# Two of eight key blocks of one query half take their bias on TensorE ahead of exp, in an attention kernel with a shared bias

## The chip, the cores and the metric

One core of a Trainium2 chip. The metric is the device time of one execution in microseconds, given as the median over several executions of one kernel; a profile's span is about 1.8 us shorter than the time of the same execution (247.7 against 249.47 us for the kernel before). Engines: PE multiplies matrices, ACT (ScalarE) does exp, DVE (VectorE) multiplies and copies, POOL (GpSimd) and SP issue transfers.

## The reference

```python
# q, k, v: [4, 8, 1024, 64] float32, bias: [1, 1, 1024, 1024] float32
scores = scale * np.matmul(q, k.transpose(0, 1, 3, 2)) + bias      # scale = 1/8
attn = exp(scores - max) / (sum(exp(scores - max)) + 1e-8)          # over the keys
return np.matmul(attn, v)
```

32 heads, and one bias for all of them. The kernel leaves the maximum out and uses exp(s + b) = exp(s) * exp(b), so that exp(b) is made once and multiplied in for every head.

## The kernel before

The scores of one head are cut into *banks* of 128 keys x 512 queries: 16 pairs of heads x 2 heads x 2 query halves x 8 key blocks = 512 banks. Three banks make a *slot*: PE fills it with three matmuls, ACT does one exp over all three. Two slots are in flight. The values' accumulators and the transposes of q and k share the two PSUM banks that remain.

```python
banks = [(pr, h, qh, kc) for pr in range(NP) for qh in range(2) for kc in range(NCH) for h in range(2)]
banks[NB - 16:] = [(NP - 1, h, 1, kc) for h in range(2) for kc in range(NCH)]
late_bias = {NB - 2: 0, NB - 1: 1}            # only these two banks get their bias on PE
slots = [[0], [1, 2]] + [list(range(i, min(i + 3, NB))) for i in range(3, NB, 3)]
# ... cut
def s_fill(g):                                # PE: scores of a slot
    # ... cut: ps is the slot's PSUM tile
    for j, b in enumerate(slots[g]):
        pr, h, qh, kc = banks[b]
        nc.tensor.matmul(ps[:, j, :], kT[:, kc, :], qT[:, h, qh * HQ:(qh + 1) * HQ],
                         start=True, stop=b not in late_bias)
        if b in late_bias:                    # adds bias / scale: identity x braw
            nc.tensor.matmul(ps[:, j, :], ident[:], braw[:, late_bias[b], :], start=False, stop=True)

def s_exp(g):                                 # ACT: exp(scale * scores) of a slot
    nc.scalar.activation(e_at(slots[g][0], n), open_ps.pop(("S", g))[:, :n, :], ACTF.Exp, scale=scale)
# b_fill / b_exp: four "bias slots" early on: PE transposes the bias, ACT makes eb = exp(bias)
def mul_pair(b, n=2):                         # DVE: E *= eb for 2 or 4 banks
    # ... cut
    nc.vector.tensor_tensor(e, e, eb[:, qh, kc:kc + 1, :].to_broadcast([P, n, HQ]), op=ALU.mult)
# av_bank: PE, four matmuls of 65 columns per bank: values and row sums
# transpose_pe: PE, eight transposes make a quarter of a pair's qT or kT; DVE copies it out (a "piece")
```

The order of all this is fixed at build time: a small list scheduler with guesses of each cost decides in which order each engine gets its instructions. Every engine then runs its own list strictly in that order. The last loads of the start are issued so:

```python
load_v(0)
for c in (QC, QC + 2):
    nc.gpsimd.dma_start(out=btraw[:, c:c + 2, :], in_=bf_[:, c:c + 2, :])   # bias of query half 1
load_qk(1)                                                                   # k and q of pair 1
load_v(1)
```

The softmax here doesn't subtract the row's maximum and nothing guards it: scores larger than these inputs give would overflow.

## Time and profile before

| | before |
|---|---|
| time, median of 3 | 249.73 us (249.12 to 250.07) |
| span of the profile | 247.7 us |
| busy: ACT, PE, DVE | 239.8, 229.4, 218.8 us |
| one exp of three banks, from end to end | 1.343 us |

Two habits of reading are needed. Busy time is a union, so the cost of one of many overlapping instructions is read from the step between neighbours, not from the mean length. And an engine whose ends are modelled (PE) looks busy while it waits. For ACT I go one step further than the page: I take the end of each activation from the trace. In the kernel before, every exp of three banks ends 1.343 us after its predecessor and each of the four bias exps 1.770, from the first three-bank exp (ends at 9.32 us) to the last slot (243.00 us). Whatever exceeds these steps I call a *stall*. A *fill* is the run of matmuls that PE issues for one slot. The lines that carry this are in the prediction.

### The profile page before, as it was taken

The page shows a single profiled execution, that of the slowest core. Times are in us where ns is not written, and L with a number is a line of the kernel's source. Part 1 is how long each engine was busy: PE and PEld are TensorE (multiplying, and loading weights), DVE is VectorE, ACT ScalarE, POOL GpSimd, SP SyncE. Part 2 cuts the span into 40 slices and gives each one's busy share as a digit, 9 for nine tenths or more (in the row PEclk, how much of TensorE's full clock was granted, in tenths as well). Part 3 has the DMA queues.
Part 4 walks back from the last instruction along what each step waited for, and adds up shares of the span by engine and source line. Part 5 has one row for each costly group of instructions (what it writes and reads, how often), then busy time and mean ns, then how long its engine had stood idle before and what let it go on. Part 6 is the DMA issues. An engine that isn't in the chain of part 4 may idle for free.

```text
span 247.7 us, 7189 instructions
## 1 busy us (share of the span) xinstructions
PE 229.4 (93%) x3153; PEld 140.9 (57%) x3153; DVE 218.8 (88%) x381; ACT 239.8 (97%) x183; POOL 54.8 (22%) x76
## 2 busy tenths in 40 slices
PE   8669999999999999999999999999999999999893
PEld 3246656656565665665656555566565555665452
DVE  4118899999999999999999999999998999998884
ACT  5899999999999999999999999999999999999993
POOL 7664534202213501303240031516000000000000
PEclk9999999999999999999999999999999999999999
DMA  6999999923925994922992049699901102020111
GB/s 116 187 202 189 200 146 192 92 85 45 149 55 101 136 81 122 91 89 30 176 132 78 17 91 123 87 130 117 127 16 42 46 0 89 3 85 3 52 57 65
DMA packets 48751, 23.79 MB, mean 96 GB/s; under 512 B 34512, under 2 KB 44624, under 8 KB 48720
## 3 DMA queue, kind: packets, MB, share of 16 engines
q0 software_dynamic: 42560, 14.42, 53.8%
q1 hardware_dynamic: 5872, 8.72, 9.8%
q8 instruction: 24, 0.39, 0.6%
q10 hardware_dynamic: 288, 0.20, 0.3%
q14 instruction: 7, 0.06, 0.1%
HBM read 29.36 MB, written 8.39 MB: 152 GB/s over the span
## 4 chain that ended last, share of the span: by engine, by line
ACT 75%; PE 12%; DVE 7%; issue 2%; DMA 2%; POOL 1%; ACTq 0%; POOLq 0%
ACT E L137 72%; PE ps L130 9%; ACT eb L150 3%; DVE E L163 2%; PE po L188 2%; DMA kr<-in_k_dram 2%; DVE E L160 1%; DVE E L157 1%; DVE oall L200 1%; PE px L89 1%; DVE qT L98 1%; DVE rs L198 0%; DVE kT L102 0%; POOL qT L260 0%; POOL qT L261 0%
## 5 line engine op out<-in xcount | busy, mean ns | idle before, releaser
L137 ACT ACTIVATE E<-ps 128x1536 bf16<-128x1536 f32 (+2 forms) x172 | 230.1, 1666 | 1.0 <-PE ps L130 1.0
L130 PE MATMUL ps<-qT,kT 128*128 128x512 bf16 x512 | 138.7, 378 | 9.8 <-ACT E L137 5.6
L188 PEld LDWEIGHTS <-E 128*128 128x128 bf16 x2016 | 82.0, 98 | 40.2 <-DVE E L160 3.8
L160 DVE TENSOR_TENSOR E<-E,eb 128x2048 bf16<-128x2048 bf16 x78 | 93.9, 1216 | 4.2 <-ACT eb L150 4.0
L188 PE MATMUL po<-vall,E 128*128 128x65 bf16 x2016 | 92.7, 194 | 2.2 <-DVE E L160 1.3
L130 PEld LDWEIGHTS <-kT 128*128 128x128 bf16 x512 | 45.0, 97 | 41.9 <-issue 10.6
L163 DVE TENSOR_TENSOR E<-E,eb 128x1024 bf16<-128x1024 bf16 x92 | 61.0, 684 | 1.9 <-ACT E L137 1.4
L75 POOL DMA_DIRECT2D kr<-in_k_dram x15 | 10.5, 701 | 87.7 <-PE px L89 85.8
L98 DVE TENSOR_TENSOR qT<-px,mask 128x1024 bf16<-128x1024 bf16 x31 | 21.3, 688 | 8.7 <-PE px L89 8.0
L81 POOL DMA_DIRECT2D vall<-in_v_dram x32 | 28.2, 884 | 3.5 <-DVE kT L317 3.1
L200 DVE TENSOR_TENSOR oall<-po,rs 128x256 f32<-128x256 f32 x63 | 26.7, 424 | 2.2
L76 POOL DMA_DIRECT2D qr<-in_q_dram x15 | 10.8, 717 | 26.2 <-PE px L89 22.8
L102 DVE COPY kT<-px 128x512 bf16<-128x512 bf16 x30 | 12.6, 420 | 1.6 <-PE px L89 1.2
L198 DVE RECIPROCAL rs<-po 128x4 f32<-128x4 f32 x63 | 11.1, 176 | 2.4 <-PE po L188 2.2
L89 PE MATMUL px<-ident,qr 128*64 128x128 bf16 x248 | 12.8, 225 | 0.0
L89 PE MATMUL px<-ident,kr 128*64 128x128 bf16 x240 | 12.4, 224 | 0.2
L89 PEld LDWEIGHTS <-qr 128*64 128x64 bf16 x248 | 7.9, 109 | 7.6 <-issue 5.1
L89 PEld LDWEIGHTS <-kr 128*64 128x64 bf16 x240 | 7.7, 109 | 6.9 <-issue 4.5
L150 ACT ACTIVATE eb<-pb 128x2048 bf16<-128x2048 bf16 x4 | 7.5, 1887 | 0.0
L145 PEld LDWEIGHTS <-btraw 128*128 128x128 bf16 x64 | 4.5, 145 | 1.5 <-issue 1.2
L145 PE MATMUL pb<-ident,btraw 128*128 128x128 bf16 x64 | 4.5, 224 | 0.8 <-ACT E L137 0.5
L157 DVE TENSOR_TENSOR E<-E,eb 128x1024 bf16<-128x1024 bf16 (+2 forms) x7 | 4.6, 686 | 0.2 <-ACT E L137 0.2
(45 smaller groups left out, 27.3 us busy)
## 6 DMA issues: line engine op xcount, KB each, us to landing
out_dram<-oall SPq DMA_DIRECT2D x28, 256.0 KB, 2.0
vall<-in_v_dram POOLq DMA_DIRECT2D x32, 128.0 KB, 5.9
kr<-in_k_dram POOLq DMA_DIRECT2D x15, 256.0 KB, 4.2
qr<-in_q_dram POOLq DMA_DIRECT2D x15, 256.0 KB, 4.8
btraw<-in_bias_dram POOLq DMA_DIRECT2D x4, 512.0 KB, 7.9
out_dram<-oall SPq DMA_DIRECT2D x7, 128.0 KB, 3.1
k0f<-in_k_dram SPq DMA_DIRECT2D x2, 128.0 KB, 3.0
q0f<-in_q_dram ACTq DMA_DIRECT2D x1, 128.0 KB, 2.5
```

The source lines that it names most:

```text
L81: nc.gpsimd.dma_start(out=vall[:, 2 * pr + t, :, :D], in_=vf[pr, :, t])
L89: nc.tensor.transpose(px[t * D:(t + 1) * D, c, :], src[:, t, half * QC + c, :], ident[:])
L98: nc.vector.tensor_tensor(dst[:, :, half * HQ:(half + 1) * HQ], px.rearrange("p c q -> p (c q)").unsqueeze(1).to_broadcast([P, 2, HQ]), ma ...
L102: nc.vector.tensor_copy(dst[:, half * QC:(half + 1) * QC, :], px[:])
L130: nc.tensor.matmul(ps[:, j, :], kT[:, kc, :], qT[:, h, qh * HQ:(qh + 1) * HQ], start=True, stop=b not in late_bias)
L137: nc.scalar.activation(e_at(slots[g][0], n), open_ps.pop(("S", g))[:, :n, :], ACTF.Exp, scale=scale)
L150: nc.scalar.activation(eb[:, qh, :, c0 * P:(c0 + 2) * P], open_ps.pop(("B", qh, c0))[:, :NCH].rearrange("p k c q -> p k (c q)"), ACTF.Exp)
L160: nc.vector.tensor_tensor(e, e, eb[:, qh, kc:kc + 2, :].unsqueeze(2).to_broadcast([P, 2, 2, HQ]), op=ALU.mult)
L163: nc.vector.tensor_tensor(e, e, eb[:, qh, kc:kc + 1, :].to_broadcast([P, n, HQ]), op=ALU.mult)
L188: nc.tensor.matmul(acc[:, i, :], e[:, 0, i * P:(i + 1) * P], vall[:, 2 * pr + h, kc, :], start=(kc == 0 and i == 0), stop=(kc == NCH - 1), ...
L198: nc.vector.reciprocal(rs[:], acc[:, :, D:D1])
L200: nc.vector.tensor_tensor(oall[:, c0:c0 + QC, :], acc[:, :, :D], rs[:].to_broadcast([P, QC, D]), op=ALU.mult)
```

## The change

Its intent: in the second query half, key blocks 6 and 7 of all heads get their bias from PE ahead of exp (an identity matmul that adds it), as the last two banks did already. exp(bias) isn't needed there, so two bias slots shrink from 8 to 6 key blocks, and DVE doesn't multiply these 64 banks. They are spread so that a slot has at most one of them until the very last slot. The cost guesses and the order of the early loads change with it.

```diff
+    NE = NCH - 2
+    for u in range(16, NB, 32):
+        early = [(u // 32, h, 1, kc) for kc in range(NE) for h in range(2)]
+        late = [(u // 32, h, 1, kc) for kc in range(NE, NCH) for h in range(2)]
... cut: the first unit also takes banks of pair 1 in, the last has its own order
+        b = u
+        while b < u + 16:
+            if late and (b % 3 == 2 and (u + 16 < NB or b < NB - 8) or not early):
+                banks[b] = late.pop(0)
+                b += 1
+            else:
+                banks[b:b + 2] = early[:2]
+                del early[:2]
+                b += 2
+    late_bias = {b: banks[b][3] - NE for b in range(NB) if banks[b][2] == 1 and banks[b][3] >= NE}
... s_fill: the bias matmuls follow the slot's three score matmuls
+        for j, b in enumerate(slots[g]):
             if b in late_bias:
                 nc.tensor.matmul(ps[:, j, :], ident[:], braw[:, late_bias[b], :], start=False, stop=True)
... b_fill and b_exp
-        nc.scalar.activation(eb[:, qh, :, c0 * P:(c0 + 2) * P],
-                             open_ps.pop(("B", qh, c0))[:, :NCH].rearrange("p k c q -> p k (c q)"), ACTF.Exp)
+        n = NE if qh else NCH
+        nc.scalar.activation(eb[:, qh, :n, c0 * P:(c0 + 2) * P],
+                             open_ps.pop(("B", qh, c0))[:, :n].rearrange("p k c q -> p k (c q)"), ACTF.Exp)
... loads
-        for c in (QC, QC + 2):
-            nc.gpsimd.dma_start(out=btraw[:, c:c + 2, :], in_=bf_[:, c:c + 2, :])
+        nc.gpsimd.dma_start(out=btraw[:, QC:QC + 2, :], in_=bf_[:, QC:QC + 2, :])
         load_qk(1)
+        nc.gpsimd.dma_start(out=btraw[:, QC + 2:, :], in_=bf_[:, QC + 2:, :])
... the scheduler's guesses
-        EXP, EXP0, QK, AV, TP = 427, 62, 216, 170, 350
+        EXP, EXP0, QK, AV, TP = 427, 62, 216, 140, 440
-        for at, x in ((3, (0, 0)), (5, (0, 2)), (9, (1, 0)), (11, (1, 2))):
+        for at, x in ((3, (0, 0)), (5, (0, 2)), (8, (1, 0)), (11, (1, 2))):
```

More of the change, by code (lines that the diff above doesn't have):

```diff
@@ L107 @@
     NB = len(banks)
-    banks[NB - 16:] = [(NP - 1, h, 1, kc) for h in range(2) for kc in range(NCH)]
-    late_bias = {NB - 2: 0, NB - 1: 1}
+    NE = NCH - 2
+    for u in range(16, NB, 32):
+        early = [(u // 32, h, 1, kc) for kc in range(NE) for h in range(2)]
+        late = [(u // 32, h, 1, kc) for kc in range(NE, NCH) for h in range(2)]
+        if u == 16:
+            early += [(1, h, 0, kc) for kc in range(NCH) for h in range(2)]
+            b = 16
+            while b < 48:
+                if late and b % 3 == 2 and b > 36:
+                    banks[b] = late.pop(0)
[4 more added lines that the diff above has]
+                    b += 2
+            continue
+        if u + 16 == NB:
+            early = [(NP - 1, h, 1, kc) for h in range(2) for kc in range(NE)]
+            late = [(NP - 1, h, 1, kc) for h in range(2) for kc in range(NE, NCH)]
+        b = u
+        while b < u + 16:
+            if late and (b % 3 == 2 and (u + 16 < NB or b < NB - 8) or not early):
+                banks[b] = late.pop(0)
+                b += 1
+            else:
+                banks[b:b + 2] = early[:2]
+                del early[:2]
+                b += 2
+    assert sorted(banks) == sorted((pr, h, qh, kc) for pr in range(NP) for h in range(2) for qh in range(2) for kc in range(NCH))
+    late_bias = {b: banks[b][3] - NE for b in range(NB) if banks[b][2] == 1 and banks[b][3] >= NE}
+    units = {}
+    for b in range(NB):
+        units.setdefault(banks[b][:3], []).append(b)
     slots = [[0], [1, 2]] + [list(range(i, min(i + 3, NB))) for i in range(3, NB, 3)]
@@ L143, in b_fill @@
         for c in range(2):
-            for kc in range(NCH):
+            for kc in range(NE if qh else NCH):
                 nc.tensor.transpose(ps[:, kc, c, :],
@@ L163, in mul_pair, with late_bias_pe @@
             nc.vector.tensor_tensor(e, e, eb[:, qh, kc:kc + 1, :].to_broadcast([P, n, HQ]), op=ALU.mult)
-    def late_bias_pe(tag):
-        px = ps_x.tile([P, 2, HQ], BF, tag=tag, name="px")
-        for j in range(2):
-            for i in range(QC):
-                nc.tensor.transpose(px[:, j, i * P:(i + 1) * P],
-                                    btraw[:, QC + i, :].rearrange("p (kp kc) -> p kc kp", kc=NCH)[:, NCH - 2 + j, :],
-                                    ident[:])
+    def late_bias_pe(j, tag):
+        px = ps_x.tile([P, HQ], BF, tag=tag, name="px")
+        for i in range(QC):
+            nc.tensor.transpose(px[:, i * P:(i + 1) * P],
+                                btraw[:, QC + i, :].rearrange("p (kp kc) -> p kc kp", kc=NCH)[:, NE + j, :], ident[:])
         def copy():
-            nc.vector.tensor_scalar(braw[:], px[:], 1.0 / scale, None, op0=ALU.mult)
+            nc.vector.tensor_scalar(braw[:, j, :], px[:], 1.0 / scale, None, op0=ALU.mult)
         return copy
@@ L182, in av_bank @@
         pr, h, qh, kc = banks[b]
-        if kc == 0:
+        first, last = (b == units[pr, h, qh][i] for i in (0, -1))
+        if first:
             po[h] = ps_x.tile([P, QC, D1], F32, tag=tag, name="po")
@@ L188, in av_bank @@
             nc.tensor.matmul(acc[:, i, :], e[:, 0, i * P:(i + 1) * P], vall[:, 2 * pr + h, kc, :],
-                             start=(kc == 0 and i == 0), stop=(kc == NCH - 1), skip_group_check=True)
-        if kc < NCH - 1:
+                             start=(first and i == 0), stop=last, skip_group_check=True)
+        if not last:
             return None
@@ L340 @@
         x_unit = {}
-        bias_at = {(0, 0): 10900, (0, 2): 13700, (1, 0): 18600, (1, 2): 20800}
-        raw_at = {0: (5900, 12600), 1: (22200, 23500), 2: (26000, 28500)}
+        bias_at = {(0, 0): 10900, (0, 2): 13700, (1, 0): 18600, (1, 2): 23300}
+        raw_at = {0: (5900, 12600), 1: (19600, 20900), 2: (26000, 28500)}
         pieces = [(0, 0, 1)]
@@ L345 @@
             pieces += [(pr, 1, 0), (pr, 0, 0), (pr, 1, 1), (pr, 0, 1)]
-        pieces.append((NP, 0, 0))
-        raw_at[NP] = (T0, T0)
+        pieces[4:4] = [(NP, 0, j) for j in range(NCH - NE)]
+        raw_at[NP] = (23400, 23400)
         piece_end = {(0, 1, 0): T0, (0, 0, 0): T0, (0, 1, 1): T0 + 200}
@@ L355 @@
         for u in range(0, NB, 16):
-            if u + 16 < NB:
-                av_order += [u + 2 * i for i in range(8)] + [u + 2 * i + 1 for i in range(8)]
-            else:
-                av_order += list(range(u, NB - 8))
+            for h in range(2):
+                av_order += units[banks[u][0], h, banks[u][2]]
+        del av_order[NB - 8:]
         av_next = 0
@@ L373, in cost_act @@
             item = order[i]
-            return EXP0 + EXP * (len(slots[item[1]]) if item[0] == "S" else 4)
+            return EXP0 + EXP * (len(slots[item[1]]) if item[0] == "S" else NE / 2 if item[1] else 4)
         def act_end_of(i):
@@ L392, in pe_fill @@
                     pr, h, qh, kc = banks[b]
-                    for key in ((pr, 1, kc // QC), (pr, 0, qh)) + (((NP, 0, 0),) if b in late_bias else ()):
+                    for key in ((pr, 1, kc // QC), (pr, 0, qh)) + (((NP, 0, late_bias[b]),) if b in late_bias else ()):
                         if key not in piece_end:
@@ L419, in pe_piece @@
             at = slots[order[i][1]][0]
-            if at < (pr - 2) * 32 + 8:
+            if pr < NP and at < (pr - 2) * 32 + 8:
                 return None
@@ L425, in pe_piece @@
             tags = sorted((x_free[x], x) for x in x_free if x != busy)
-            if busy and left < 4 and at < pr * 32 - 16:
+            if busy and left < 4 and pr < NP and at < pr * 32 - 16:
                 return None
-            if not busy and av_next and at < pr * 32 - 16 and tags[0][0] + SEM < t_pe and len(tags) > 1 and tags[1][0] > t_pe:
+            if not busy and av_next and pr < NP and at < pr * 32 - 16 and tags[0][0] + SEM < t_pe and len(tags) > 1 and tags[1][0] > t_pe:
                 return None
@@ L431, in pe_piece @@
             ready = max(free + SEM, raw_at[pr][1 - which])
-            cost_t = TP if pr < NP else 720
+            cost_t = TP
             def emit(t):
                 pieces.pop(0)
-                copy = transpose_pe(pr, which, half, tag) if pr < NP else late_bias_pe(tag)
-                cost = COPYK if which else COPYQ
+                copy = transpose_pe(pr, which, half, tag) if pr < NP else late_bias_pe(half, tag)
+                cost = COPYK if which or pr == NP else COPYQ
                 x_free[tag] = 1e12
@@ L500, in pe_av @@
             u = unit_of(b)
-            if banks[b][3] == 0:
+            if b == units[u][0]:
                 free, tag = min((x_free[x], x) for x in x_free)
@@ L521, in pe_pick @@
             f = pe_fill()
+            bare = not f and len(filled) < NO and order[len(filled)][0] == "S"
             best = None
@@ L530, in pe_pick @@
                 limit = max(act_end_of(i - 2) + SEM, act_end_of(i - 1) - 830)
-            for c in (pe_piece(), pe_av()):
+            for is_av, c in enumerate((pe_piece(), pe_av())):
                 if c is None:
@@ L534, in pe_pick @@
                 start = max(t_pe, c[0])
-                if start + pe_cost(start, c[1]) > limit and not force:
+                if start + pe_cost(start, c[1]) > limit and not force and (is_av or not bare):
                     continue
@@ L551, in dve_pick @@
                     ready = max(exp_at[b + n - 1], eb_at[(qh, kc)]) + SEM
-                    if n == 2 and b % 4 == 0 and b + 3 in exp_at and (qh, kc + 1) in eb_at and b + 3 not in late_bias and \
+                    if n == 2 and b >= 32 and b % ET <= ET - 4 and [x[1:] for x in banks[b:b + 4]] == \
+                            [(y, qh, kc + x) for x in range(2) for y in range(2)] and b + 3 in exp_at and (qh, kc + 1) in eb_at and b + 3 not in late_bias and \
                             exp_at[b + 3] + SEM <= max(t_dve, ready) and \
@@ L566, in run @@
                         mul_next += n
+                        while mul_next in late_bias:
+                            mul_next += 1
                     c.append((ready, 2, cost, run))
```

## The prediction

> **What bounds the kernel now.** I read the engine totals first, then the slices, then the groups, and then the order of time, because a share of busy time does not say which engine the others wait for.
>
> ```profile
> PE 229.4 (93%) x3153; PEld 140.9 (57%) x3153; DVE 218.8 (88%) x381; ACT 239.8 (97%) x183; POOL 54.8 (22%) x76
> ...
> PE   8669999999999999999999999999999999999893
> ...
> DVE  4118899999999999999999999999998999998884
> ACT  5899999999999999999999999999999999999993
> ...
> L137 ACT ACTIVATE E<-ps 128x1536 bf16<-128x1536 f32 (+2 forms) x172 | 230.1, 1666 | 1.0 <-PE ps L130 1.0
> L130 PE MATMUL ps<-qT,kT 128*128 128x512 bf16 x512 | 138.7, 378 | 9.8 <-ACT E L137 5.6
> L188 PE MATMUL po<-vall,E 128*128 128x65 bf16 x2016 | 92.7, 194 | 2.2 <-DVE E L160 1.3
> L160 DVE TENSOR_TENSOR E<-E,eb 128x2048 bf16<-128x2048 bf16 x78 | 93.9, 1216 | 4.2 <-ACT eb L150 4.0
> L163 DVE TENSOR_TENSOR E<-E,eb 128x1024 bf16<-128x1024 bf16 x92 | 61.0, 684 | 1.9 <-ACT E L137 1.4
> ```
>
> Three engines show nines nearly everywhere, but only ACT has no idle time: its 172 exps of scores sat idle before for 1.0 us in all, and that was in the first 8 us. The score matmuls on PE wait for ACT (5.6 us), hardly ACT for PE. The mean of 1666 ns is not the price of an exp, since one overlaps the next; the price is the step in the chain of waits, read in order of time (start, us, what):
>
> ```profile
> 13.35 1.77 ACT eb L150
> 15.12 1.34 ACT E L137
> 16.46 1.77 ACT eb L150
> 18.23 4.03 ACT E L137 x3
> 22.26 1.77 ACT eb L150
> 24.03 1.34 ACT E L137
> 25.38 1.77 ACT eb L150
> ```
>
> An exp of three score banks takes 1.34 us, an exp of a bias slot (2048 elements) 1.77 us. From 9.3 us to the end of the last exp at 243.0 us the sum is 168 x 1.343 (three banks) + 4 x 1.77 + 0.92 (the last slot, two banks) = 233.6: the stretch itself. There is not a tenth of a microsecond of slack on ACT to win back. What follows, 243.0 to 247.7, is the last attention-value matmuls, a division and the output DMA.
>
> PE is less full than its 93% looks, since the ends of matmuls are modelled. In the order of time:
>
> ```profile
> 99.74 0.81 PE L130 MATMUL ps<-qT,kT 128*128 128x512 bf16 x3
> 100.38 0.66 PE L188 MATMUL po<-vall,E 128*128 128x65 bf16 x16
> 101.08 0.81 PE L130 MATMUL ps<-qT,kT 128*128 128x512 bf16 x3
> 101.73 0.65 PE L188 MATMUL po<-vall,E 128*128 128x65 bf16 x16
> 102.43 0.81 PE L130 MATMUL ps<-qT,kT 128*128 128x512 bf16 x3
> ```
>
> The fills start 1.34 us apart, which is ACT's step. A score matmul costs (0.81 - 0.378)/2 = 0.2155 us of issue, an attention-value matmul (0.66 - 0.194)/15 = 0.031, so three plus sixteen are 1.15 us of 1.34, and the rest is PE waiting for a score slot.
>
> **What the Trainium skill says.** "ScalarE: Activation LUTs", section Rules for kernel authors, budgets about 0.83 ns per element plus about 0.3 us per ACTIVATE. The slope agrees: (1.77 - 1.34)/512 = 0.84 ns. The fixed part doesn't: 1.343 - 1536 x 0.83 leaves 0.07 us here. "TensorE: Matmul & The Clock Gate", section Back-to-back issue gap, gives about 216 ns for an isolated 512-column matmul and about 131 in a stream with weight loads; this trace has 0.2155 us in such a stream, so I use that. "PSUM — Partial Sum Buffer", Specifications (TRN2), has 8 banks of 512 fp32. The kernel's two score slots of three banks and two accumulators take all 8, so a fill may begin only when the exp two slots back is done, and no third slot can hide a longer fill. "VectorE: DVE Perf Modes", the section Side-by-side, gives about 1224 ns for a two-input op on 2048 bf16; the trace has 1216.
>
> **The change, part by part.** The order of instructions of both kernels, compared engine by engine, gives the counts.
>
> *ACT.* 172 score exps as before. Two of the four bias exps shrink from 2048 to 1536 elements, the shape of a score exp, so each falls from 1.77 to 1.34: 2 x 0.43 = **0.86 us off the path**. Nothing else leaves ACT.
>
> *DVE.* Multiplies of four banks go from 79 to 43, of two banks from 96 to 137: 510 banks to 448. By the union of busy time, 93.9/78 = 1.204 and 61.0/92 = 0.663 us each: 95.1 + 63.6 = 158.7 before, 51.8 + 90.8 = 142.6 after. **DVE sheds 16 us**, 219 to about 203, all beside ACT's chain. Fewer than one eighth of the cost goes because 2-bank multiplies cost more per bank (0.33 against 0.30).
>
> *PE.* The bias matmuls go from 2 to 64, so 62 x 0.2155 = 13.4 us more; eight bias transposes fewer give back 8 x 0.061 = 0.5. **PE gains 12.9 us.** A q or k piece (eight transposes) costs 0.44 us with its two changes of kind: 0.35 from its first matmul to the next kind, plus 0.09 more than usual ahead of it. Over the slots from the first value matmul to the last but one, contents average 1.196 us before and 1.277 after, of a slot's 1.343: from 89% to 95%.
>
> The average doesn't decide; the worst slots do. From the order, a slot with bias plus a piece is 4 x 0.2155 + 0.44 = 1.31; bias plus 12 value matmuls 1.24; bias plus 16 is 1.36 (13 slots, 0.02 over); bias, piece and 4 is 1.43 (7 slots, 0.09 over); bias, piece and 8 is 1.56 (2 slots, 0.21 over). Bias never shares a slot with 20. After each overfull one a lighter slot follows, so the running excess never exceeds 0.25 us after the start. In the kernel before the same sum peaks at 0.25 in steady state too (two slots of 3 scores, 16 value matmuls and a piece, 1.59 us), and there the exps keep their step of 1.34. The new order is the evener one.
>
> The fill itself lengthens from 0.81 to 4 x 0.2155 + 0.16 = 1.03 us when it has a bias. It must fit in one step of 1.34. The kernel before shows a longer fill that fits: 16 bias transposes took 1.15 us, from 12.06 to 13.21, and the bias exp that needed them came at its turn, at 13.35 in the chain. That leaves at least 0.12 us for a fill that starts late.
>
> *Head.* Key and query of pair 1 are now loaded ahead of the last bias megabyte, and scores of pair 1 are needed from bank 28 on. The second bias exp of half 1 fills when the score exp two before it ends, 18.23 + 4 x 1.343 = 23.6; in the kernel before the load in that place of the queue had landed at about 23.0 (the query of pair 1, first used at 23.50). DVE must do six 2-bank multiplies at 0.60 apart, a copy (0.42) and the masked copy of q (0.69) from 18.27 on, which ends at about 22.9; the two score matmuls that need it then end near 23.5, for an exp due at 23.6. Both margins are thin; if they break, the loss is once, 0.1 to 0.5 us.
>
> *Tail.* The last 16 banks end as before: both last banks already took their bias on PE. No change expected in the 4.7 us after the last exp.
>
> Sum: 249.73 - 0.86 + about 0.15 for a thin head or a rare late fill = **249.0 us**.
>
> **The rivals.** (1) *PE becomes the bound.* For it: 12.9 us more on an engine at 93% busy; if all of it came on the path, 262 us. Against: the real issue load is 89%, and becomes 95%. If PE added waits on DVE that use up the 5%, perhaps 251 to 254. (2) *The longer fill misses its exp.* Two score slots leave 1.34 us per fill; if the 62 fills with a bias each came 0.1 us late, 6 us: about 255. Against it, the 1.15 us fill of bias transposes that fits. (3) *DVE was the hidden bound*, as the nines of its slices suggest, and shedding 16 us makes the kernel 2 to 5% faster, 238 to 245. Against: ACT has no idle time to give, and its count of score exps is unchanged; this can't go under about 248.5. (4) *The shrunk bias exps buy nothing* because the head waits on the bias load: 249.5 to 250.
>
> **Range and chances.** Three runs before spread over 0.95 us, which alone is about half of what I expect to gain. The floor is 249.1 - 0.86 = 248.3 for a lucky median; a handful of late fills makes 250.3. So 248.3 to 250.4. Faster than 2% (under 244.7) needs ACT work that isn't removed: 0.01. Slower than 2% (over 254.7) needs rival 2, or 1 at a third of its weight: 0.04.
>
> **What would show it.** In the changed kernel's profile: ACT's busy time near 239 and its idle time before the score exps still about 1 us; the chain of waits with two bias exps of 1.34 instead of 1.77; fills with bias still 1.34 us apart in mid-kernel, 0.216 longer; DVE at about 203 us; the last exp ending near 242.1. Wrong would be: score exps waiting on PE for several us (rival 1 if after slots with pieces, rival 2 if after every slot with a bias), or a gap on ACT near 23 to 26 us (the head).

## The result

The changed kernel took 248.74 us (248.36 to 249.19, 6 runs) against 249.76 us (249.12 to 250.4, 6 runs) of the kernel before. The ratio is 0.9958, 95% interval 0.9939 to 0.9977. (Ratios are the mean time of one kernel's fast runs over the mean of the other's in the same rounds, so not quite the ratio of the medians quoted.) On another chip job (e10 below) it was 248.62 against 249.44, ratio 0.9971 (0.9949 to 0.9992).

The page's totals and slices of the changed kernel:

```profile
PE 232.0 (94%) x3155; PEld 143.4 (58%) x3207; DVE 206.8 (84%) x387; ACT 239.2 (97%) x183; POOL 54.8 (22%) x76
...
PE   8767999999999999999999999999999999999893
...
DVE  5128799999999898998989899897979989896883
ACT  5999999999999999999999999999999999999993
```

DVE's row of nines has broken into eights and sevens: it has time now, 12 us of it. ACT's row is as full as it was. PE got 13.4 us of new matmuls, and its busy time rose by 2.6 only. That is too little even for a modelled busy time: this trace lacks records (see below). The trace of e8, which has every record and the same work on PE, reads 235.2, so the rise is about 5.8. That the rest fills what had counted as busy while PE waited is argued.

The costliest groups of the changed kernel (line, engine, operation, shapes, count, busy us, mean ns, idle before and its releaser):

```profile
L172 ACT ACTIVATE E<-ps 128x1536 bf16<-128x1536 f32 (+2 forms) x172 | 230.1, 1535 | 0.8 <-PE ps L164 0.8
L164 PE MATMUL ps<-qT,kT 128*128 128x512 bf16 x460 | 135.7, 378 | 6.1 <-ACT E L172 1.5
L199 DVE TENSOR_TENSOR E<-E,eb 128x1024 bf16<-128x1024 bf16 x132 | 88.5, 685 | 10.0 <-ACT E L172 4.8
L196 DVE TENSOR_TENSOR E<-E,eb 128x2048 bf16<-128x2048 bf16 x43 | 52.2, 1217 | 1.1 <-ACT E L172 0.9
L168 PE MATMUL ps<-braw,ident 128*128 128x512 bf16 x64 | 24.1, 379 | 0.0
L186 ACT ACTIVATE eb<-pb 128x2048 bf16<-128x2048 bf16 (+1 forms) x4 | 6.7, 1675 | 0.0
```

The score exps are the same 230.1 us as before; the bias exps went from 7.5 to 6.7. (The trace lacks 52 of the 512 score matmuls: their weight loads are all there, and the results are right.) The mean length of an exp has become a reading of its own. It was 1666 ns and is 1535; since one ends every 1.343 us in both, an exp now starts 0.19 us ahead of its predecessor's end on average instead of 0.32. The fills come closer to the deadline, and still make it.

A fill with a bias matmul, in the changed kernel's timeline of PE (start us, us, what, count):

```profile
27.80 0.82 PE L164 MATMUL ps<-qT,kT 128*128 128x512 bf16 x3
28.46 0.38 PE L168 MATMUL ps<-braw,ident 128*128 128x512 bf16 x1
28.67 0.53 PE L223 MATMUL po<-vall,E 128*128 128x65 bf16 x12
29.15 0.81 PE L164 MATMUL ps<-qT,kT 128*128 128x512 bf16 x3
```

The bias matmul takes 0.21 us from its start to the next kind's, and the fills remain 1.35 us apart.

Where time was lost is only visible at the start. ACT's timeline there:

```profile
17.41 2.81 ACT L172 ACTIVATE E<-ps 128x1536 bf16<-128x1536 f32 x2
20.07 1.49 ACT L186 ACTIVATE eb<-pb 128x1536 bf16<-128x1536 bf16 x1
21.77 1.45 ACT L172 ACTIVATE E<-ps 128x1536 bf16<-128x1536 f32 x1 [0.21 <-PE ps L164]
23.49 1.45 ACT L172 ACTIVATE E<-ps 128x1536 bf16<-128x1536 f32 x1 [0.27 <-PE ps L164]
24.96 1.45 ACT L186 ACTIVATE eb<-pb 128x1536 bf16<-128x1536 bf16 x1
```

The two shrunk bias exps (128x1536) are there and step like a score exp. But three steps in a row are too long: from end to end 1.66, 1.72 and 1.47 us, so 0.32 + 0.38 + 0.13 = 0.83 us of stalls. The chain of waits, which ran over ACT in the kernel before, runs here over a transfer:

```profile
11.49 12.43 DMA btraw<-in_bias_dram
23.93 0.04 issue
23.97 0.95 PE pb L180 x12
```

The last bias megabyte landed at 23.93 us. After the bias exp that it releases there is no stall at all: the step of 1.343 us holds to the last slot.

So the two profiled executions differ by this ledger (us; the second column is the end of the first three-bank exp, and the body is everything on ACT from there to the last exp, without stalls):

| trace | first exp ends | body | stalls before 31 us | later stalls | after the last exp | span |
|---|---|---|---|---|---|---|
| before | 9.32 | 233.67 | 0 | 0 | 4.71 | 247.71 |
| changed | 8.61 | 232.82 | 0.83 | 0 | 4.66 | 246.92 |

The body is 0.85 shorter, which is the two bias exps. That the execution of the changed kernel was 0.71 us earlier at the first exp isn't the change's doing: nothing ahead of that point differs, and in 14 traces of both kernels and their variants this point falls anywhere from 8.61 to 10.73 us. In this trace the early start and the stalls about cancel; that is not so in every trace (e10 below).

### The profile page after: what moved, and what is told of

The parts are those of the page before. It is cut to its first block, busy times and chain, and to the rows that moved or that the text cites. A ratio compares the mean times of both kernels' runs of the same rounds, so it can differ in the third digit from the quotient of the medians.

```text
span 246.9 us, 7261 instructions
## 1 busy us (share of the span) xinstructions
PE 232.0 (94%) x3155; PEld 143.4 (58%) x3207; DVE 206.8 (84%) x387; ACT 239.2 (97%) x183; POOL 54.8 (22%) x76
## 4 chain that ended last, share of the span: by engine, by line
PE 79%; ACT 9%; DMA 5%; DVE 3%; POOL 1%; issue 1%; ACTq 0%
PE ps L164 41%; PE po L223 23%; ACT E L172 9%; PE px L89 8%; DMA btraw<-in_bias_dram 5%; PE ps L168 5%; PE ps L309 1%; DVE E L199 1%; POOL vall L81 1%; DVE oall L235 1%; DVE E L193 0%; PE pb L180 0%; PE px L319 0%; POOL qr L76 0%; POOL kr L75 0%
## 5 line engine op out<-in xcount | busy, mean ns | idle before, releaser
L172 ACT ACTIVATE E<-ps 128x1536 bf16<-128x1536 f32 (+2 forms) x172 | 230.1, 1535 | 0.8 <-PE ps L164 0.8
L164 PE MATMUL ps<-qT,kT 128*128 128x512 bf16 x460 | 135.7, 378 | 6.1 <-ACT E L172 1.5
L223 PEld LDWEIGHTS <-E 128*128 128x128 bf16 x2016 | 79.3, 98 | 33.8 <-DVE E L199 2.1
L199 DVE TENSOR_TENSOR E<-E,eb 128x1024 bf16<-128x1024 bf16 x132 | 88.5, 685 | 10.0 <-ACT E L172 4.8
L223 PE MATMUL po<-vall,E 128*128 128x65 bf16 x2016 | 87.4, 194 | 1.5 <-DVE E L196 0.8
L164 PEld LDWEIGHTS <-kT 128*128 128x128 bf16 x512 | 44.0, 96 | 31.1 <-issue 4.7
L196 DVE TENSOR_TENSOR E<-E,eb 128x2048 bf16<-128x2048 bf16 x43 | 52.2, 1217 | 1.1 <-ACT E L172 0.9
L168 PE MATMUL ps<-braw,ident 128*128 128x512 bf16 x64 | 24.1, 379 | 0.0
L168 PEld LDWEIGHTS <-ident 128*128 128x128 bf16 x64 | 6.2, 97 | 7.6
L186 ACT ACTIVATE eb<-pb 128x2048 bf16<-128x2048 bf16 (+1 forms) x4 | 6.7, 1675 | 0.0
```

The lines of the kernel that those rows point to most:

```text
L196: nc.vector.tensor_tensor(e, e, eb[:, qh, kc:kc + 2, :].unsqueeze(2).to_broadcast([P, 2, 2, HQ]), op=ALU.mult)
L223: nc.tensor.matmul(acc[:, i, :], e[:, 0, i * P:(i + 1) * P], vall[:, 2 * pr + h, kc, :], start=(first and i == 0), stop=last, skip_group_c ...
```

## The experiments

Each was timed in five rounds beside the kernel before. Four at a time share one set of runs of before: medians 249.31 (e1 to e4), 249.37 (e5 to e8) and 249.44 us (e9 to e12).

The ledger of all traces, with the body left out (232.8 us with shrunk bias exps, 233.7 without). As above, the last slot, of two banks, is outside the stalls; in e5 and e6 it was late as well, by 0.31 and 0.09 us:

| trace | time, median | ratio to before (95%) | first exp ends | stalls before 31 us | later stalls | span |
|---|---|---|---|---|---|---|
| e1 | 249.41 | 0.9997 (0.9982 to 1.0013) | 9.01 | 0.01 | 0 | 247.41 |
| e2 | 248.92 | 0.9981 (0.9962 to 0.9999) | 8.91 | 0.40 | 0 | 246.85 |
| e3 | 249.57 | 1.0007 (0.9987 to 1.0027) | 9.33 | 0.15 | 0 | 247.83 |
| e4 | 248.56 | 0.9964 (0.9946 to 0.9982) | 8.92 | 0.94 | 0 | 247.33 |
| e5 | 258.63 | 1.0363 (1.0339 to 1.0386) | 9.46 | 0.63 | 9.79 | 257.61 |
| e6 | 253.61 | 1.0163 (1.0139 to 1.0186) | 8.84 | 0.28 | 4.59 | 251.21 |
| e7 | 252.08 | 1.0110 (1.0087 to 1.0134) | 8.70 | 0.08 | 3.99 | 250.19 |
| e8 | 248.45 | 0.9959 (0.9938 to 0.9979) | 9.18 | 0.08 | 0 | 246.73 |
| e9 | 249.61 | 0.9999 (0.9985 to 1.0013) | 8.92 | 0.08 | 0.96 | 247.42 |
| e10 | 248.62 | 0.9971 (0.9949 to 0.9992) | 9.20 | 0.08 | 0 | 246.76 |
| e11 | 248.63 | 0.9974 (0.9953 to 0.9995) | 10.73 | 0.09 | 0 | 248.29 |
| e12 | 250.18 | 1.0035 (1.0004 to 1.0066) | 9.32 | 1.25 | 0 | 248.04 |

### e1: the kernel before without the multiplies of the 64 banks

```diff
         pr, h, qh, kc = banks[b]
+        if qh and kc >= NCH - 2:
+            return
+        if qh and n > 1 and banks[b + 1][1] == h:
+            n = min(n, NCH - 2 - kc)
```

> The kernel before, with the multiplies of the 64 banks (key blocks 6 and 7 of the second half) left out and nothing put in their place: wrong result on purpose. DVE sheds about 20 us, nothing else moves. My theory (ACT alone sets the time, DVE relief is worth nothing): 249.7 us, ratio to before within 0.998 to 1.002, and every exp still ends 1.343 us after the last. Rival (DVE was a hidden bound and part of the 1.0 us gain is its relief): 249.2 or less, ratio 0.998 or lower.

249.41 us, ratio 0.9997, no stall. DVE's busy time falls from 218.8 to 202.7 us in the trace, 16 us instead of the 20 expected, and nothing changes, so the gain isn't DVE's relief.

### e2: the same, and the two bias exps shrunk

```diff
-            for kc in range(NCH):
+            for kc in range(NCH - 2 if qh else NCH):
                 nc.tensor.transpose(ps[:, kc, c, :], ...
+        n = NCH - 2 if qh else NCH
-        nc.scalar.activation(eb[:, qh, :, ...], open_ps.pop(...)[:, :NCH] ...
+        nc.scalar.activation(eb[:, qh, :n, ...], open_ps.pop(...)[:, :n] ...
```

> As e1, and the two bias exps of the second half shrunk to 1536 elements as well (wrong on purpose): the ACT part of the change alone, in the old order of loads and slots. My theory: 0.86 us less than before, 248.9 us, ratio 0.9965, no stall of ACT near 20 to 26 us, because the old load order is kept. Rival (DVE relief pays too): 248.4 or less. Rival (the head is held by the bias load anyway, shrinking buys little): 249.4 or more.

248.92 us, but the ratio is 0.9981, half of the gain that I expected (0.9965 is still inside the interval). The trace has the body shorter by 0.85 as it should, and stalls of 0.12, 0.16 and 0.13 us between 27 and 30 us that the kernel before doesn't have. They fit its order: just ahead of these stalls PE has a slot with three scores, a piece and 20 value matmuls, and in this trace its fill at 24.67 us is followed by the next at 26.39, 1.72 us later. A bias exp of 1.77 covers that; one of 1.34 doesn't. So shrinking alone gave about half of itself back in the old order. That this slot is the reason is argued; no run isolated it.

### e3: the changed kernel with full bias exps

```diff
-            for kc in range(NE if qh else NCH):
+            for kc in range(NCH):
-        n = NE if qh else NCH
+        n = NCH
```

> The changed kernel, but its two later bias exps (and their transposes) keep all 2048 elements. If ACT alone sets the head: 0.86 us slower than the changed kernel, 249.6. If the head of the changed kernel is held by the landing of the last bias megabyte (last exp of the bias not before about 25 us whatever ACT does), the first longer exp fits in the wait: only 0.43 to 0.6 slower, 249.2, and the stalls of 0.32, 0.38 and 0.13 us that the changed kernel's trace shows ahead of its 13th to 15th long activation become smaller.

249.57 us, ratio 1.0007: the whole gain is gone, as far as the times tell (0.9958 and 0.9971 with the shrink). The trace has both things that I had set against each other: the body is 0.85 longer, and the stalls are down to 0.15 us. But the longer exp need not be what shrank them: in this trace the key of pair 1 landed at 17.97 us instead of 20.52 (see e10). How much of the shrink a given execution keeps depends on its stalls at the start.

### e4: the changed kernel without its bias matmuls

```diff
-        for j, b in enumerate(slots[g]):
-            if b in late_bias:
-                nc.tensor.matmul(ps[:, j, :], ident[:], braw[:, late_bias[b], :], start=False, stop=True)
```

> The changed kernel in its own order, but the 64 bias matmuls on PE are not issued (wrong on purpose): PE sheds 13.8 us, fills fall from 1.03 back to 0.81 us. My theory: PE's added work is all in its spare time, so no change against the changed kernel, 248.7 us (248.4 to 249.0). Rival (the longer fills or the fuller slots cost something, and the gain would be larger without): 248.3 or less, and score exps whose end-to-end step was over 1.343 in the changed kernel come back to it.

248.56 us, beside 248.62 and 248.74 of the changed kernel. Its trace has the stalls of the start, 0.94 us, and none later, just as with the matmuls. The 13.8 us of PE work cost nothing where they are.

### e5 and e6: bias matmuls issued twice

Both run in the changed kernel's order, with right results; e6 doubles one of the two key blocks only.

```diff
             if b in late_bias:
-                nc.tensor.matmul(ps[:, j, :], ident[:], braw[:, late_bias[b], :], start=False, stop=True)
+                n = 2 if True else 1              # e6: if late_bias[b] == 0
+                for i in range(n):
+                    nc.tensor.matmul(ps[:, j, :], ident[:], braw[:, late_bias[b], :], start=False, stop=i == n - 1)
... and braw holds half the bias where it is added twice
```

> The changed kernel in its own order, each bias matmul issued twice with half the bias (right result): 64 x 0.2155 = 13.8 us more on PE, longest fill 5 x 0.2155 + 0.16 = 1.24 us. The average slot content on PE becomes 1.358 us against 1.343 of ACT; the running sum of excess over 1.343 along the order peaks at 5.96 us, of which about 0.3 is absorbed. My theory (PE costs nothing until its slots overflow, then all of it): about 5.6 us slower than the changed kernel, 254.3 us (252.5 to 255.5). Rival (only the share of busy time counts, PE still under the span in sum): under 250.

> As e5, but only one of the two bias blocks is issued twice: 32 x 0.2155 = 6.9 us more on PE, average slot content 1.317 of 1.343, running excess peaks at 0.76 us. My theory: 0.76 less about 0.3 that the score slots absorb, so 0.4 us slower than the changed kernel, 249.1 (248.7 to 249.5). Rival (PE load costs in proportion): half of what e5 costs, 2 us or more.

258.63 and 253.61 us, where I had expected 254.3 and 249.1. Both expectations fell, and e6's the more tellingly: no running excess of PE's work alone explains 4.9 us of stalls. The stalls have a pattern. The slots with a bias come in groups, mostly four in a row, and the first doubled slot of a group is late by 0.09 us in nearly every group of both runs (0.13 to 0.15 in the others). A fill of five matmuls that starts as soon as its slot is free therefore takes 1.343 + 0.092 us until its exp can keep the step, and 1.435 - 5 x 0.2155 leaves 0.357 us that isn't issue: from the end of the exp that frees the slot to the first matmul, and from the last matmul's issue to the exp that uses it. I had counted 0.16 for that. With 0.357, four matmuls need 1.219 us and have 0.12 to spare, five are 0.09 late, six 0.31.

These first slots make up about 1.5 us of e6's stalls. The other 3.2 us fall on the slots behind them, 0.07 to 0.31 each, where PE is still at other work when the slot comes free; so in e6 the fill and the load act together. An estimate: replaying the order of PE's instructions in e6's trace with the prediction's costs, from slot 20 to the last but one and without waits for DVE, gives 3.95 us of stalls with 0.357 and 1.3 with 0.16; the trace has 4.1 there.

### e7: the same bias matmuls, not spread

```diff
-                if late and b % 3 == 2 and b > 36:
+                if late and not early:
-            if late and (b % 3 == 2 and (u + 16 < NB or b < NB - 8) or not early):
+            if late and (b % 3 == 2 and u + 16 == NB and b < NB - 8 or not early):
```

> The changed kernel with the same 64 bias matmuls, but not one per slot: the four bias banks of a half stand together, so 11 slots carry three of them and 9 carry two. A fill of three score and three bias matmuls takes 6 x 0.2155 + 0.16 = 1.45 us, over the 1.343 that two score slots leave. Theory that the fill's length counts: 11 slots x about 0.2 us late, 250.9 us (250.2 to 251.8), with steps of 1.5 to 1.6 us at those slots and nowhere else after the head. Rival (only the load of PE counts, spreading is decoration): 248.7 as the changed kernel.

252.08 us, a little over the expected range: 3.99 us of stalls, of which 3.58 are at the 11 slots with three bias matmuls, 0.31 to 0.36 each. The timeline of the first of them:

```profile
31.17 0.81 PE L164 MATMUL ps<-qT,kT 128*128 128x512 bf16 x3
31.81 0.81 PE L168 MATMUL ps<-braw,ident 128*128 128x512 bf16 x3
32.55 0.41 PE L89 MATMUL px<-ident,qr 128*64 128x128 bf16 x8
32.66 4.13 ACT L172 ACTIVATE E<-ps 128x1536 bf16<-128x1536 f32 x3 [0.20 <-PE ps L168]
```

The fill takes from 31.17 to 32.62 (the last bias matmul's modelled end), and ACT, idle for 0.20, starts at 32.66. From end to end this step is 0.307 us too long, and the account of e5 says 6 x 0.2155 + 0.357 - 1.343 = 0.307. The rest of the slots fits too: of the eight slots with two bias matmuls that stand in pairs, the first of each pair is 0.09 us late, as five matmuls should be, and the second adds nothing, since the exp before it was late by as much. This timeline also shows what the 0.357 is made of: 0.05 from the end of the exp that freed the slot (31.12) to the first matmul, 0.20 from the last matmul's issue (32.46) to the exp, and 0.11 because an exp that finds ACT idle takes 1.45 us instead of a step of 1.343. The work of PE is the same as in the changed kernel; where it lies differs (the scheduler orders the other instructions anew around it).

### e9: as much load, but outside the fills

```diff
+        for i in range(QC if kc == 3 else 0):
+            nc.tensor.matmul(acc[:, i, :], zeros[:], vall[:, 2 * pr + h, kc, :], start=False, stop=False,
+                             skip_group_check=True)
         for i in range(QC):
             nc.tensor.matmul(acc[:, i, :], e[:, 0, ...
```

> The changed kernel in its own order, with 63 x 4 value matmuls by a block of zeros added among the value matmuls (right result): 252 x 0.031 = 7.8 us more on PE, more than the 6.9 us of e6, but no fill is longer. A new theory, from e5 to e7: a fill of n matmuls ahead of an exp is late by n x 0.2155 + 0.357 - 1.343 us if positive (4: 0.12 to spare; 5: 0.09 late; 6: 0.31 late), plus what PE is behind when the slot comes free. By it the mid-kernel stalls sum to 0.8 us here, 249.4 to 249.7 us, against 4.9 in e6. Rival (the load of PE is what cost e6 its 4.9 us): 4.9 us of stalls or more, 253.5.

249.61 us, later stalls 0.96 us where the account said 0.8, with 7.8 us more on PE; e6 had lost 4.59 us (4.68 with its last slot) for 6.9. ACT's group in e6, and then in e9:

```profile
L174 ACT ACTIVATE E<-ps 128x1536 bf16<-128x1536 f32 (+2 forms) x172 | 233.7, 1467 | 1.9 <-PE ps L170 0.6
```

```profile
L172 ACT ACTIVATE E<-ps 128x1536 bf16<-128x1536 f32 (+2 forms) x172 | 231.0, 1472 | 0.4 <-PE ps L164 0.4
```

The union of ACT's busy time grows with the stalls (a late exp overlaps its predecessor less), so its share stays at 97% in both; idle time alone would have hidden most of e6's loss. Neither e7 nor this run was used to fit the 0.357, so they are the tests of it: at an unchanged load longer fills cost 4 us, and more load outside the fills costs 1.

### e8, e11 and e10: one load moved, beside the changed kernel

```diff
-        load_v(0)
+        nc.gpsimd.dma_start(out=vall[:, 0, :, :D], in_=vf[0, :, 0])
         nc.gpsimd.dma_start(out=btraw[:, QC:QC + 2, :], in_=bf_[:, QC:QC + 2, :])
         load_qk(1)
         nc.gpsimd.dma_start(out=btraw[:, QC + 2:, :], in_=bf_[:, QC + 2:, :])
+        nc.gpsimd.dma_start(out=vall[:, 1, :, :D], in_=vf[0, :, 1])
```

> The changed kernel with one load moved: the v of the second head of pair 0 (first used at about 28.7 us) is issued after the last bias load instead of ahead of the key of pair 1. Key, query and last bias should land about 1.0 us earlier (20.5, 21.5, 23.9 become 19.5, 20.5, 22.9). My theory that the head stalls (0.83 us in the changed kernel's trace) are waits for these three landings: they shrink to 0.2 or less, 248.0 us (247.7 to 248.4). Rival (they are PE or DVE order, not landings): stalls stay at 0.6 or more, 248.7.

e8 took 248.45 us with 0.08 us of stalls in its trace, as hoped, but its ratio of 0.9959 is the changed kernel's own (0.9958). So both ran again on one chip:

> e8 again beside the changed kernel: head stalls of 0.1 us or less against 0.4 to 0.9, so 0.3 to 0.8 us faster than e10, 248.2 us. If the two medians are within 0.1 us of each other, the head stalls do not matter in most executions and e8's trace was a lucky one.

> The changed kernel itself, beside e11 on the same chip: 248.7 us, head stalls of 0.4 to 0.9 us in its trace, none later.

248.63 and 248.62 us: no difference, and both expectations fell, e10's 0.4 to 0.9 us of stalls included. The changed kernel's second trace, e10, shows why. ACT's timeline:

```profile
20.67 1.47 ACT L186 ACTIVATE eb<-pb 128x1536 bf16<-128x1536 bf16 x1
22.00 2.91 ACT L172 ACTIVATE E<-ps 128x1536 bf16<-128x1536 f32 x2
24.81 1.44 ACT L186 ACTIVATE eb<-pb 128x1536 bf16<-128x1536 bf16 x1
```

Here the stalls came to 0.08 us in all. PE's transposes of pair 1's key, in the first trace of the changed kernel and in e10:

```profile
20.56 0.41 PE L89 MATMUL px<-ident,kr 128*64 128x128 bf16 x8 [0.59 <-DMA kr<-in_k_dram]
20.50 0.41 PE L89 MATMUL px<-ident,kr 128*64 128x128 bf16 x8
```

In the first trace PE waited for this load, in e10 it didn't. By the landings in the traces, pair 1's key was there at 20.52 us in the first and at 18.11 in e10, the last bias megabyte at 23.93 and 22.61. Among the eight traces with this order of loads, three had the key at 20.5 to 21.2 us and stalls of 0.5 to 0.9 us at the start (the changed kernel, e4, e5); five had it at 18.0 to 19.5 and 0.08 to 0.15 us up to 27 us (e3, e6, e7, e9, e10). It isn't the moment of the first exp that decides: it ended at 8.92 us in both e4 and e9, with 0.94 and 0.08 us of stalls. What makes the same loads land earlier or later is not known. e8's landings (key 18.27, last bias 22.05 us) are like e10's, so its few stalls can't be credited to the moved load. The moved load is worth nothing measurable; I have no version that beats the changed kernel. The late e11 trace (first exp at 10.73 us) is the time of 250.08 among its runs.

### e12: the changed kernel with the old order of loads

```diff
-        load_qk(1)
         nc.gpsimd.dma_start(out=btraw[:, QC + 2:, :], in_=bf_[:, QC + 2:, :])
+        load_qk(1)
```

> The changed kernel with the old order of loads (the last bias megabyte ahead of key and query of pair 1). Key and query of pair 1 then land about 2.5 us later (near 22 and 23.3 us instead of 20.5 and 21.5), while scores of pair 1 are still needed from bank 28 on, whose exp is due at about 23 us. My theory: stalls of 1.5 to 2.5 us at that exp and the one before it, 1 to 1.7 us slower than the changed kernel, 250.1 us. Rival (the order of loads doesn't matter, later activations absorb it): 248.9 or less.

250.18 us, as expected, 1.6 us slower than e10, with stalls of 0.69 and 0.56 us at two exps that start before 25 us (1.25 us, where I had expected 1.5 to 2.5). The key of pair 1 was transposed at 21.64 and its query at 22.92 us, each after a wait for its load. The reordered loads are a necessary part of the change: the new order of banks needs pair 1 early.

## Why the prediction was right

248.74 us was within 248.3 to 250.4 and 0.26 from the 249.0 predicted. The number alone proves little: the interval of the ratio spans a gain of 0.6 to 1.5 us. The prediction calls a scatter of 0.95 us "about half" of the gain that it expects; it is more than that gain. A few of its slot sums are 0.01 off (1.31, 1.24, 1.56 and 1.59 should be 1.30, 1.23, 1.55 and 1.58), and nothing rests on that. Point by point:

- **ACT sets the time; 0.86 us leave it.** Shown. The body of the trace is 0.85 shorter in every variant with the shrink (the changed kernel, e2, e4) and as before in those without (e1, e3), and e3 loses the gain.
- **DVE's relief is worth nothing (rival 3).** Shown by e1. Its size was off: 206.8 us busy instead of 203. The multiplies had about the predicted price (0.67 and 1.21 us by the union); with more idle time between them instructions overlap less, which is argued and was not tested.
- **PE takes 12.9 us more beside the path (rival 1).** Shown by e4, and e9 shows that even 7.8 us more cost only 1.0.
- **The longer fill fits (rival 2).** Right, with the "at least 0.12 us" taken from the fill of 16 bias transposes: the reserve by the account of e5 is 1.343 - 4 x 0.2155 - 0.357 = 0.12. The bound was sound; that it was all there is was chance. But the term "4 x 0.2155 + 0.16 = 1.03 us" was mis-sized: the time outside the issue is 0.357, so 1.22. Believing 1.03, I expected five matmuls to fit (e5, e6), and they don't. The prediction gave the sums of the slots the deciding part and the fill a supporting one; e7 and e9 show the reverse. The running excess of up to 0.25 was harmless since it meets fills of three, which have 0.34 to spare: in e8's trace, which has every record, fills of three start up to 0.20 us later than the 0.05 after the slot comes free, fills of four at most 0.09 (from slot 20 on).
- **The head.** "Both margins are thin; if they break, the loss is once, 0.1 to 0.5 us" was right in kind, and the profiled execution even showed the "gap on ACT near 23 to 26 us" that the prediction had named as a sign of being wrong. The exp that needs the masked copy of q is 0.08 us late in most traces of the new order (in e10 its fill waits 0.5 us for that copy). The loads cost 0.83 us in one trace of the changed kernel and nothing in the other. The landing of the last bias was put at 23.0; it was 23.93 in the one and 22.61 in the other. A step was missing: the transposes of pair 1's key stand ahead of a fill that doesn't need them, so that fill waits for the key's load too.
- **The tail.** 4.66 instead of 4.71 us after the last exp: no change, as said.

## What to carry to other kernels

When one engine is saturated, count first what leaves that engine: 16 us fewer on DVE (e1) and 13.8 more on PE (e4) were both worth nothing measurable, 0.86 us on ACT was the gain. With two buffers between producer and consumer, the producer's fill plus the handover on both sides must fit in one step of the consumer, and this limit can bite at a load that is harmless when it is spread (e7); spread extra work one piece per buffer. Judge head effects from several traces: with the same order of loads, the stalls at the start were 0.08 us in one and 0.94 in another.

## What the Trainium skill lacked or had wrong

- "ScalarE: Activation LUTs", Rules for kernel authors: the slope per element holds (0.83 ns), but the row's fixed part of about 0.3 us is not what an exp costs in a stream: 0.07 us, from 1.343 us for 1536 elements in every step of the kernel before; an exp that found ACT idle took 1.45 us, so 0.17. The row is a budget for one ACTIVATE; the page's section What ACT_TABLE_LOAD costs does say that ACTIVATEs back to back overlap, so nothing is wrong there, but the row alone misleads.
- "TensorE: Matmul & The Clock Gate", Back-to-back issue gap: 131 ns per 512-column matmul in a stream with weight loads is not seen; it is 0.2155 us, the page's figure for the isolated gap. Nor are its 81 ns for 128 columns: the transposes of the bias, each a weight load and a matmul of 128 columns, step by 0.060 us.
- "PSUM — Partial Sum Buffer" tells how many banks there are, but not the cost of handing one over: between ACT's release of a slot and the exp of its next contents in full step lie 0.357 us besides the matmuls' issue (fitted on e5 and e6, tested by e7 and e9).
- No page that I used says that the start varies from execution to execution: the first three-bank exp ended between 8.61 and 10.73 us in 14 traces, and in the eight with the changed order of loads the key of pair 1 landed 7.1 to 10.4 us after its issue.
